# Block transposes over 128 partitions with a trip through HBM, in a float32r two-block transformer kernel

## The chip, the cores and the metric

The kernel runs on one core of a Trainium2 chip. The metric is the device time of one execution in microseconds; for the kernel before it is the median of three runs. Five engines take part, each with its own instruction queue: TensorE (PE; its weight loads are listed apart as PEld), VectorE (DVE), ScalarE (ACT), GpSimd (POOL) and SyncE (SP). SP, ACT and POOL also issue transfers, which all run on the same 16 DMA engines.

## The reference, cut to what matters

The input is one sequence of 256 tokens by 1024 channels, float32. It passes through two blocks of two layers each. Every layer of either block has the same frame:

```python
for l in range(2):
    x = x + 0.5 * swiglu(rms_norm(x, ffn1_norm[l]), ffn1_w_in[l], ffn1_w_out[l])
    x = x + mixer(rms_norm(x, mix_norm[l]), ...)
    x = x + 0.5 * swiglu(rms_norm(x, ffn2_norm[l]), ffn2_w_in[l], ffn2_w_out[l])

def swiglu(x, w_in, w_out):
    g, u = jnp.split(x @ w_in, 2, axis=-1)
    return (jax.nn.silu(g) * u) @ w_out
```

The FFN is 1024 to 2 x 2816 to 1024. The mixers differ: in the first block (mixer1 below) neighbourhood attention with a bias and a two-dimensional Fourier mix, both gated; in the second (mixer2) stick-breaking attention, compressed, selected and windowed attention, and top-k attention. So there are eight FFNs, two mixer1 and two mixer2.

## The kernel before, in words

The 256 tokens are two tiles of 128 (`T = 2`). A product `h @ w` has the tokens on the output's partitions: the activations are the stationary operand and must stand with channels on the partitions, so every activation that enters a product is first transposed. The weights are the moving operand, 512 columns at a time.

Float32 accuracy is had by splitting: `split` (L313) makes `hi`, a value rounded to float32r by ScalarE, and `lo = value - hi` by VectorE. `mm3` (L112) does three matmuls, hi x hi, hi x lo, lo x hi (L114, L115, L116).

`dense` (L118) is a product over `nk` slabs of 128 channels. For every four slabs it calls `unit` (L80), which issues one weight transfer of 1 MB on SP into one of four `raw` buffers and splits it in two pairs of slabs (tiles `whi` and `wlo` of 2 x 512 columns; two buffers in pools of their own and, in FFNs and mixer1, two more in the pool `big`, in mixer2 one more). A pair feeds 2 slabs x 2 token tiles x 3 = 12 matmuls.

Work that need not come at once is put in a list, `todo`: after each weight pair's split, `unit` takes up to `rate` entries off the list (L104 to L106), with the order kept behind that split; `drain` (L61) does the rest. The final order on each engine is set by a scheduler that goes by its own estimates, so that the list's order shifts somewhat.

`ffn` (L218): six chunks `c`, each with the gate and the up product (the sixth has both in one), then ScalarE's Silu out of the accumulators (`sl`, L246) and VectorE's product into `h` (L248). There are three accumulator buffers beside the four for attention, so the next chunk's matmuls need the evacuations. Chunks are grouped (0-1, 2-3, 4, 5); at a group's end `queue_t` (L65) puts the group's transposes on the list: 1024 columns (`nk = 8`) twice, then 512, then 256 for each token tile. `queue_blocks` (L179) makes 16 VectorE transposes for each token tile, each of one 32-partition row of blocks into 32 partitions of `hT`:

```python
hv[32 * qc : 32 * qc + 32, :, t * P + 32 * qa : t * P + 32 * qa + 32],
src[32 * qa : 32 * qa + 32, :nk, qc, :]
```

Then follow splits of `hT` into `hhi`, `hlo`, the stationary operands of the two output products (L252 on). After the first of these, half of `x` is final and is transposed in the same way by `queue_x` (L170); the other half goes over TensorE (`xt_half`, L187). `mixer1` (L432 on) does it for q and k (`qT`, `kT`). Mixer2 transposes on TensorE only, but for `queue_x` of its neighbours.

POOL has little to do: some memsets and the loads of small broadcast operands, among them the gate bias `h` in mixer1 (L518).

Of the kernel before, what the change touches and what calls it, by code (L numbers as in the profile page):

```python
# [10 lines left out]
F32 = mybir.dt.float32  # L11
# [7 lines left out]
P = 128  # L19
T = 2  # L20
# [6 lines left out]
class Net:  # L27
    def __init__(self, tc, ctx, a):
        self.tc, self.nc, self.a = tc, tc.nc, a
        nc = self.nc  # L30
        pool = lambda n, b, **kw: ctx.enter_context(tc.tile_pool(name=n, bufs=b, **kw))
# [9 lines left out]
        self.at = pool("at", 4, space=PS)  # L41
        self.tp = pool("tp", 1, space=PS)
        self.uid = 0
        self.flip = False
# [13 lines left out]
        self.hold = False  # L58
        self.todo, self.rate = [], 4

# [4 lines left out]
    def queue_t(self, h, nk, hhi, hlo, k0):  # L65
        hv = self.b("hT", n=2048)[:, : nk * 256].rearrange("p (k t) -> p k t", k=nk)
        for t in range(T):
            self.queue_blocks(h[t], nk, hv, t)
        for i in range(0, nk, 2):
            self.todo.append(lambda i=i: self.split(hhi[:, k0 + i : k0 + i + 2], hlo[:, k0 + i : k0 + i + 2],  # L70
                                                    hv[:, i : i + 2]))

# [97 lines left out]
    def queue_x(self, li):  # L170
        nc = self.nc
        hv = self.xtile()[:, :1024].rearrange("p (k t) -> p k t", k=4)
        for t in range(T):
            self.queue_blocks(self.x[:, t, :512], 4, hv, t)
        for k in range(4):
            g = self.gcol[:, li, k : k + 1] if isinstance(li, int) else li[:, k : k + 1]
            self.todo.append(lambda k=k, g=g: self.split(self.xhi[:, k], self.xlo[:, k], hv[:, k], scale=g))

    def queue_blocks(self, src, nk, hv, t):  # L179
        src = src.rearrange("p (k c i) -> p k c i", c=4, i=32)  # L180
        for q in range(16):
            qa, qc = q // 4, q % 4
            self.todo.append(lambda qa=qa, qc=qc: self.nc.vector.transpose(  # L183
                (hv(qc) if callable(hv) else hv)[32 * qc : 32 * qc + 32, :, t * P + 32 * qa : t * P + 32 * qa + 32],
                src[32 * qa : 32 * qa + 32, :nk, qc, :]))

# [196 lines left out]
class Mix1:  # L383
# [34 lines left out]
    def mixer1(self, l, nxt):  # L418
        nc, a, tc = self.nc, self.a, self.tc
# [3 lines left out]
        big = self.big  # L423
        self.more(2)
        tl = lambda n, sh, dt=F32: big.tile(sh, dt, name=self.nm(n), tag="m1" + n)
        kzh = big.tile([P, 4, 2, 256], F32R, name=self.nm("kzh"), tag="mlo")
        kq = big.tile([P, 4096], F32R, name=self.nm("kq"), tag="m1th")
        kzl = kq[:, :2048].rearrange("p (k i t) -> p k i t", k=4, i=2)
        ql = kq[:, 2048:3072].rearrange("p (k t) -> p k t", k=4)
        qT = big.tile([P, 4, 256], F32, name=self.nm("qT"), tag="m1fhi")  # L430
        kT = big.tile([P, 4, 256], F32, name=self.nm("kT"), tag="m1flo")
        qh, vn = tl("qh", [P, 4, 256], F32R), tl("vn", [P, T, 512])  # L432
# [6 lines left out]
        for c in range(4):  # L439
# [5 lines left out]
            if c < 2:  # L445
                h = []
                for t in range(T):
# [6 lines left out]
                    h.append(ht)  # L454
                for t in range(T):
                    self.queue_blocks(h[t], 4, qT if c == 0 else kT, t)
            elif c == 2:
# [12 lines left out]
        self.drain()  # L470
        self.split(qh, ql, qT)
        for i in range(2):
            r = slice(64 * i, 64 * i + 64)
            self.split(kzh[r, :, i, :], kzl[r, :, i, :], kT[r])
        ohi, olo = tl("ohi", [P, 4, 256], F32R), tl("olo", [P, 4, 256], F32R)
# [19 lines left out]
        for g in range(4):  # L495
            pa = self.psum(self.at)
            for tt in range(T):
                s = slice(g * P, (g + 1) * P)
# [5 lines left out]
            for q in range(2):  # L504
                s = slice(q * P, (q + 1) * P)
# [9 lines left out]
        for c in range(4):  # L515
# [4 lines left out]
            for t in range(T):  # L520
                d = th[:, t, c * 512 : (c + 1) * 512]
# [20 lines left out]
class Mix2:  # L542
    def consts2(self):
        nc, a = self.nc, self.a
# [9 lines left out]
        nc.scalar.dma_start(out=self.mc32[:, P:], in_=a["c2m"][:, 0:P])  # L554
        self.c2v = self.cst2.tile([P, 286], F32, name="c2v")
        nc.scalar.dma_start(out=self.c2v, in_=a["c2v"])
        v = self.c2v
# [6 lines left out]
        self.bmask = v[0:120, 278:286]  # L564
        self.one = self.cst2.tile([P, 1], F32, name="one")
        nc.gpsimd.memset(self.one, 1.0)
# [72 lines left out]
    def compress(self, l, kv, z, hid):  # L639
        nc, a = self.nc, self.a  # L640
# [19 lines left out]
        nc.tensor.transpose(ph[:, P : P + 30], th, self.ident[:30, :30])  # L660
        hT = self.b("chT", 30)
        nc.vector.tensor_copy(hT, ph[:, P : P + 30])
# [4 lines left out]
    def mixer2(self, l, nxt):  # L667
        nc, a = self.nc, self.a
# [4 lines left out]
        big = self.big  # L673
# [3 lines left out]
        tl = lambda n, sh, dt=F32, tag=None, bufs=1: big.tile(sh, dt, name=self.nm(n), tag=tag or "m2" + n, bufs=bufs)  # L677
# [16 lines left out]
        nc.gpsimd.memset(ikz, 0.0)  # L694
        kcz = tl("kcz", [P, 2, 15])
        nc.gpsimd.memset(kcz, 0.0)
# [134 lines left out]
        def cmp(t):  # L831
            sc = self.psum(self.at)
            for p in range(4):
                mm(sc[:, p * 30 : (p + 1) * 30], lhsT=nq[:, p, t * P : (t + 1) * P], rhs=flat(kcz), start=True, stop=True)
            pr = self.b("cpr", 120)
            pv3 = pr.rearrange("p (h c) -> p h c", h=8)
# [131 lines left out]
        for nm_, o, kk in (("a", oa, 2), ("b", ob, 4), ("c", oc, 2)):  # L968
# [4 lines left out]
            hi, lo = hl[:, :kk], hl[:, kk:]  # L973
# [6 lines left out]
        for n in range(2):  # L980
            for i, nm_ in enumerate("abc"):
                hi, lo, kk = oT[nm_]
                y = self.dense(hi, lo, kk, [(a[f"w_br_{nm_}_2"][l], n * 512, 512)])
                for t in range(T):
                    d, d0 = th[2 * i + n][:, t], th[n][:, t]
# [154 lines left out]
```

## Time and profile before

| | |
|---|---|
| median of 3 runs | 2369.55 us (2368.86 to 2369.81) |
| span of the profiled execution | 2366.5 us, first to last instruction |
| PE / PEld busy | 2291.0 us (97%) / 1846.8 us (78%) |
| DVE busy | 1891.9 us (80%) |
| ACT busy | 1144.7 us (48%) |
| POOL busy | 22.3 us (1%) |
| weight queue (q1) | 397.44 MB, 51.0% of 16 DMA engines' span |
[...]

The span is that of one execution on the chip; its own time is not listed apart from the three runs, whose lowest is 2.4 us above the span. Matmuls are pipelined: each is listed with some 390 ns while the next starts 227 ns after it, so a busy TensorE says that there was no gap longer than that overlap, and start-to-start distances say more. Times in the rows are microseconds unless marked ns. "A <- B: us, times, longest" in the view of waits says how long A's engine stood before A until B ended.

### The profile page before, as it was taken

The page shows a single profiled execution, that of the slowest core. Times are in us where ns is not written, and L with a number is a line of the kernel's source. Part 1 is how long each engine was busy: PE and PEld are TensorE (multiplying, and loading weights), DVE is VectorE, ACT ScalarE, POOL GpSimd, SP SyncE. Part 2 cuts the span into 40 slices and gives each one's busy share as a digit, 9 for nine tenths or more (in the row PEclk, how much of TensorE's full clock was granted, in tenths as well). Part 3 has the DMA queues.
Part 4 walks back from the last instruction along what each step waited for, and adds up shares of the span by engine and source line. Part 5 has one row for each costly group of instructions (what it writes and reads, how often), then busy time and mean ns, then how long its engine had stood idle before and what let it go on. Part 6 is the DMA issues. An engine that isn't in the chain of part 4 may idle for free.

```text
span 2366.5 us, 28600 instructions
## 1 busy us (share of the span) xinstructions
PE 2291.0 (97%) x10446; PEld 1846.8 (78%) x10446; DVE 1891.9 (80%) x3797; ACT 1144.7 (48%) x1632; POOL 22.3 (1%) x47
## 2 busy tenths in 40 slices
PE   8999999999999999999999999999999999999999
PEld 7777788778778788777777887787787788778777
DVE  6898866896798876798788896768958978877785
ACT  5444445445444455445444655544444455455443
POOL 0000000000000000000000000000000000000000
PEclk9999999999999999999999999999999999999999
DMA  7555555556546645546555544455464555325553
GB/s 257 177 171 185 177 170 178 173 174 201 182 151 200 191 152 178 189 142 219 176 175 179 174 125 132 137 185 182 166 211 161 173 191 156 124 96 189 185 177 117
DMA packets 228269, 407.07 MB, mean 172 GB/s; under 512 B 20800, under 2 KB 46016, under 8 KB 228128
## 3 DMA queue, kind: packets, MB, share of 16 engines
q1 hardware_dynamic: 212272, 397.44, 51.0%
q10 hardware_dynamic: 14944, 4.79, 0.9%
q0 software_dynamic: 912, 3.02, 0.5%
q8 instruction: 82, 1.34, 0.2%
q14 instruction: 59, 0.48, 0.1%
HBM read 404.16 MB, written 1.05 MB: 171 GB/s over the span
## 4 chain that ended last, share of the span: by engine, by line
PE 66%; DVE 27%; issue 5%; ACT 2%; DMA 1%; ACTq 0%; DVEq 0%
PE ps L115 20%; PE ps L116 20%; PE ps L114 19%; DVE hT L183 14%; DVE wlo L316 8%; DVE h L248 2%; PE ps L377 2%; DVE hlo L316 1%; ACT whi L315 1%; PE ps L370 1%; PE ps L863 1%; DVE qT L183 1%; PE ps L655 1%; DMA raw<-in_mix_w_in_dram 1%; PE ps L194 1%
## 5 line engine op out<-in xcount | busy, mean ns | idle before, releaser
L315 ACT CAST whi<-raw 128x1024 fp32r<-128x1024 f32 (+2 forms) x754 | 780.2, 1043 | 834.4 <-PE ps L116 744.8
L316 DVE TENSOR_TENSOR wlo<-raw,whi 128x1024 fp32r<-128x1024 f32 (+2 forms) x754 | 907.6, 1213 | 337.1 <-ACT whi L315 323.6
L115 PE MATMUL ps<-wlo,xhi 128*128 128x512 f32 (+2 forms) x2048 | 804.6, 394 | 14.7 <-DVE wlo L316 14.7
L114 PE MATMUL ps<-whi,xhi 128*128 128x512 f32 (+2 forms) x2048 | 772.4, 394 | 22.1 <-DVE h L248 18.9
L116 PE MATMUL ps<-whi,xlo 128*128 128x512 f32 (+2 forms) x2048 | 791.2, 390 | 0.0
L114 PEld LDWEIGHTS ps<-whi,xhi 128*128 128x128 f32 x2048 | 383.4, 188 | 112.7 <-DVE h L248 25.7
L115 PEld LDWEIGHTS ps<-wlo,xhi 128*128 128x128 f32 x2048 | 384.8, 188 | 110.5 <-DVE wlo L316 31.2
L116 PEld LDWEIGHTS ps<-whi,xlo 128*128 128x128 f32 x2048 | 384.8, 188 | 79.3 <-issue 0.5
L183 DVE STREAM_TRANSPOSE hT<-h 32x256 f32<-32x256 f32 (+2 forms) x1024 | 360.8, 352 | 15.4
L115 PE MATMUL ps<-wlo,hhi 128*128 128x512 f32 x704 | 279.1, 396 | 23.7 <-DVE wlo L316 23.7
L116 PE MATMUL ps<-whi,hlo 128*128 128x512 f32 x704 | 275.8, 392 | 0.0
L114 PE MATMUL ps<-whi,hhi 128*128 128x512 f32 x704 | 266.2, 392 | 1.1 <-DVE h L248 0.2
L115 PEld LDWEIGHTS ps<-wlo,hhi 128*128 128x128 f32 x704 | 132.1, 188 | 65.2 <-DVE wlo L316 37.5
L114 PEld LDWEIGHTS ps<-whi,hhi 128*128 128x128 f32 x704 | 132.2, 188 | 33.7 <-DVE h L248 4.6
L116 PEld LDWEIGHTS ps<-whi,hlo 128*128 128x128 f32 x704 | 132.2, 188 | 27.8
L315 ACT CAST hhi<-hT 128x512 fp32r<-128x512 f32 x88 | 49.1, 618 | 119.1 <-DVE hT L183 119.1
L246 ACT ACTIVATE sl<-ps,rstd 128x512 f32<-128x512 f32 (+1 forms) x96 | 62.3, 651 | 56.4 <-PE ps L116 52.3
L183 DVE STREAM_TRANSPOSE hT<-x 32x128 f32<-32x128 f32 x224 | 67.7, 302 | 3.4
L365 ACT ACTIVATE pr<-ms,nmx 128x256 f32<-128x256 f32 (+1 forms) x112 | 51.3, 461 | 34.0 <-DVE nmx L360 29.9
L248 DVE SCALAR_TENSOR_TENSOR h<-ps,rstd,sl 128x512 f32<-128x512 f32 (+1 forms) x96 | 64.7, 700 | 1.9 <-PE ps L116 1.6
L316 DVE TENSOR_TENSOR hlo<-hT,hhi 128x512 fp32r<-128x512 f32 x88 | 55.7, 685 | 0.3
L137 ACT ACTIVATE jk<-x 128x512 f32<-128x512 f32 x52 | 32.7, 630 | 5.3 <-DVE x L299 2.6
(350 smaller groups left out, 1681.7 us busy)
## 6 DMA issues: line engine op xcount, KB each, us to landing
raw<-in_ffn_w_gu_dram SPq DMA_DIRECT2D x80, 1024.0 KB, 5.1
raw<-in_ffn_w_in_dram SPq DMA_DIRECT2D x79, 1024.0 KB, 5.2
raw<-in_ffn_w_out_dram SPq DMA_DIRECT2D x40, 1024.0 KB, 5.0
raw<-in_ffn_w_down_dram SPq DMA_DIRECT2D x40, 1024.0 KB, 5.1
raw<-in_mix_w_in_dram SPq DMA_DIRECT2D x32, 1024.0 KB, 6.7
raw<-in_w_gate_dram SPq DMA_DIRECT2D x24, 1024.0 KB, 5.1
raw<-in_w_in_dram SPq DMA_DIRECT2D x12, 1024.0 KB, 5.5
raw<-in_ffn_w_in_dram SPq DMA_DIRECT2D x16, 512.0 KB, 4.6
```

The costliest lines, as they stand in the source:

```text
L114: mm(ps[:, :n], lhsT=lh, rhs=hi, start=start, stop=False)
L115: mm(ps[:, :n], lhsT=lh, rhs=lo, start=False, stop=False)
L116: mm(ps[:, :n], lhsT=ll, rhs=hi, start=False, stop=stop)
L137: self.nc.scalar.activation(junk, self.x[:, t, n * 512 : (n + 1) * 512], AF.Square, accum_out=ss[:, t, n : n + 1])
L183: self.todo.append(lambda qa=qa, qc=qc: self.nc.vector.transpose((hv(qc) if callable(hv) else hv)[32 * qc : 32 * qc + 32, :, t * P + 32 * ...
L194: nc.tensor.transpose(ps[:, j * 256 + t * P : j * 256 + (t + 1) * P], self.x[:, t, k * P : (k + 1) * P], self.ident)
L246: nc.scalar.activation(sl[:, :w], gs[t][:, :w], AF.Silu, scale=rs[:, t : t + 1])
L248: nc.vector.scalar_tensor_tensor(h[t][:, o : o + w], us[t][:, :w], rs[:, t : t + 1], sl[:, :w], op0=ALU.mult, op1=ALU.mult)
L315: self.nc.scalar.copy(hi, src)
L316: return self.nc.vector.tensor_sub(lo, src, hi.bitcast(F32))
L365: nc.scalar.activation(pr[:, s], src[:, s], AF.Exp, bias=nm[:, j : j + 1], accum_out=den[:, j : j + 1])
L377: nc.tensor.matmul(po[:, j * 64 : (j + 1) * 64], lhsT=pt[:, q], rhs=v(j, st), start=(st == 0), stop=(st == ns - 1))
```

## The change

- `queue_blocks` is gone. `turned` takes its place: for each token tile one VectorE transpose over all 128 partitions, which turns each 32 x 32 block in place and gathers the columns so that element `i` of a block is column `4 i + c` (the input steps by 4 elements). The result goes to `hB`, one buffer. After the second token tile, POOL issues a store of `hB` to a buffer in HBM (`hop`, two for each size) and a load back into the tile, which brings the rows to their partitions.
- Splits read the loaded tile in pieces of 32 columns; there are as many as before for 1024 and 512 columns, one more for 256; `queue_x` has 8 of 128 columns instead of 4 of 256; q has 2 in place of 1, k 4 in place of 2.
- Two empty entries (three in `queue_x`) stand in the list between the transposes and the splits, and `rate` is 1 instead of 4.
- Tiles of odd size are padded: `c2v` 286 to 288 columns, `one` 1 to 16, `kcz` 30 to 32, `chT` 30 to 32, `cpr` 120 to 128.

```diff
+        self.hop = pool("hop", 2, space=bass.MemoryType.DRAM)
...
-        self.todo, self.rate = [], 4
+        self.todo, self.rate = [], 1
...
     def queue_t(self, h, nk, hhi, hlo, k0):
-        hv = self.b("hT", n=2048)[:, : nk * 256].rearrange("p (k t) -> p k t", k=nk)
-        for t in range(T):
-            self.queue_blocks(h[t], nk, hv, t)
-        for i in range(0, nk, 2):
-            self.todo.append(lambda i=i: self.split(hhi[:, k0 + i : k0 + i + 2], hlo[:, k0 + i : k0 + i + 2],
-                                                    hv[:, i : i + 2]))
+        hv = self.turned(lambda t: h[t], nk, self.b("hT", n=2048))
+        self.todo += [lambda: None] * 2
+        step = min(nk, 4)
+        for i in range(0, nk, step):
+            for t in range(T):
+                o = lambda d: d[:, k0 + i : k0 + i + step, t * P : (t + 1) * P].rearrange(
+                    "p k (q j) -> p k q j", j=32)
+                self.todo.append(lambda hi=o(hhi), lo=o(hlo), s=hv[:, i : i + step, t]: self.split(hi, lo, s))
+
+    def turned(self, src, nk, tile):
+        nc = self.nc
+        n = nk * 256
+        hop = self.hop.tile([4, P, nk * 64], F32, name=self.nm("hop"), tag=f"hop{nk}")
+        hb = self.b("hB", n=2048, bufs=1)[:, :n]
+        ov = hb.rearrange("p (c k t j) -> p k c t j", c=4, t=T, j=32)
+
+        def turn(t):
+            nc.vector.transpose(ov[:, :, :, t, :], src(t)[:, : nk * P].rearrange("p (k i c) -> p k c i", c=4, i=32))
+            if t == T - 1:
+                nc.gpsimd.dma_start(out=hop.rearrange("q (i c) n -> (q i) (c n)", c=4), in_=hb)
+                nc.gpsimd.dma_start(out=tile[:, :n].rearrange("p (q n) -> p q n", q=4),
+                                    in_=hop.rearrange("q p n -> p q n"))
+
+        self.todo += [lambda t=t: turn(t) for t in range(T)]
+        return tile[:, :n].rearrange("p (q k t j) -> p k t q j", q=4, t=T, j=32)
...
     def queue_x(self, li):
...
+        hv = self.turned(lambda t: self.x[:, t, :512], 4, self.xtile())
+        self.todo += [lambda: None] * 3
...
-        self.c2v = self.cst2.tile([P, 286], F32, name="c2v")
-        nc.scalar.dma_start(out=self.c2v, in_=a["c2v"])
+        self.c2v = self.cst2.tile([P, 288], F32, name="c2v")
+        nc.scalar.dma_start(out=self.c2v[:, :286], in_=a["c2v"])
...
-        self.one = self.cst2.tile([P, 1], F32, name="one")
+        self.one = self.cst2.tile([P, 16], F32, name="one")[:, :1]
```

How it moves instructions, at two places. First VectorE in the first FFN, at the end of chunk 1: `h` are the chunk's two evacuations, `wlo` the low halves of the next weight pairs, `hlo` the low half of the transposed group. Before:

```order
L248 SCALAR_TENSOR_TENSOR h_333<-ps_411,rstd_304,sl_481 128x512
L248 SCALAR_TENSOR_TENSOR h_334<-ps_412,rstd_304,sl_484 128x512
L183 STREAM_TRANSPOSE hT_487<-h_333 32x8x32 x12
L316 TENSOR_TENSOR wlo_543<-raw_532,whi_542 128x1024
L183 STREAM_TRANSPOSE hT_487<-h_333 32x8x32 x4
L316 TENSOR_TENSOR wlo_579<-raw_576,whi_578 128x1024
L183 STREAM_TRANSPOSE hT_487<-h_334 32x8x32 x4
```

And now:

```order
L263 SCALAR_TENSOR_TENSOR h_335<-ps_413,rstd_306,sl_483 128x512
L263 SCALAR_TENSOR_TENSOR h_336<-ps_414,rstd_306,sl_486 128x512
L84 STREAM_TRANSPOSE hB_491<-h_335 128x8x4x32
L331 TENSOR_TENSOR wlo_539<-raw_532,whi_538 128x1024
L84 STREAM_TRANSPOSE hB_491<-h_336 128x8x4x32
L331 TENSOR_TENSOR wlo_571<-raw_568,whi_570 128x1024
L331 TENSOR_TENSOR wlo_577<-raw_568,whi_576 128x1024
L331 TENSOR_TENSOR wlo_609<-raw_606,whi_608 128x1024
L331 TENSOR_TENSOR wlo_615<-raw_606,whi_614 128x1024
L331 TENSOR_TENSOR wlo_657<-raw_654,whi_656 128x1024
L331 TENSOR_TENSOR hlo_151<-hT_489,hhi_150 128x4x128 x4
```

Thirty-two transposes in bursts of twelve and four became two, and five weight pairs stand between the second and the splits. On ScalarE the casts `hhi` of the same group stand, as before, in the middle of the weight casts:

```order
L330 CAST whi_614<-raw_606 128x1024
L261 ACTIVATE sl_649<-ps_493,rstd_306 128x512
L330 CAST whi_656<-raw_654 128x1024
L330 CAST hhi_150<-hT_489 128x4x128 x4
L330 CAST whi_660<-raw_654 128x1024
```

What they wait for is no longer VectorE but the load into `hT`. That load stands on POOL's queue, which holds now, for the first FFN and on into mixer1:

```order
L86 DMA hop_490<-hB_491 128x2048
L87 DMA hT_489<-hop_490 128x4x512
L86 DMA hop_799<-hB_800 128x2048
L87 DMA hT_798<-hop_799 128x4x512
L86 DMA hop_962<-hB_963 128x1024
L87 DMA hT_961<-hop_962 128x4x256
L86 DMA hop_1049<-hB_1050 128x512
L87 DMA hT_1048<-hop_1049 128x4x128
L86 DMA hop_1257<-hB_1258 128x1024
L87 DMA hT_1256<-hop_1257 128x4x256
```

Each load waits on POOL for its store; before, POOL had nothing at this place.

## Rows read from the trace of the kernel before

**Rows 1.** The page, part 1: busy us, share of the span, instructions.

```profile
PE 2291.0 (97%) x10446; PEld 1846.8 (78%) x10446; DVE 1891.9 (80%) x3797; ACT 1144.7 (48%) x1632; POOL 22.3 (1%) x47
```

**Rows 2.** Waits, whole span: us in total, times, longest us.

```profile
ACT whi L315 <- PE ps L116: 744.8, 485, 7.1
...
PE ps L115 <- DVE wlo L316: 38.4, 57, 1.7
...
PE ps L114 <- DVE h L248: 19.0, 17, 1.2
```

**Rows 3.** Chain of waits in 97 to 128 us, shares by line.

```profile
by line: DVE hT L183 44.4%; DVE wlo L316 19.7%; issue 13.9%; DVE hlo L316 8.0%; DVE h L248 6.4%; ACT whi L315 3.4%; PE ps L114 2.4%; PE ps L116 1.5%; PE ps L115 0.8%
```

**Rows 4.** Timeline of DVE from 97 us: start us, us, what.

```profile
99.44 1.40 DVE L248 SCALAR_TENSOR_TENSOR h<-ps,rstd,sl 128x512 f32<-128x512 f32 x2
100.76 5.36 DVE L183 STREAM_TRANSPOSE hT<-h 32x256 f32<-32x256 f32 x12
106.15 1.23 DVE L316 TENSOR_TENSOR wlo<-raw,whi 128x1024 fp32r<-128x1024 f32 x1
107.41 1.80 DVE L183 STREAM_TRANSPOSE hT<-h 32x256 f32<-32x256 f32 x4
```

**Rows 5.** Timeline of PE, a stretch without waits in either block's FFN.

```profile
590.02 0.39 PE L114 MATMUL ps<-whi,xhi 128*128 128x512 f32 x1
...
602.03 0.39 PE L116 MATMUL ps<-whi,xlo 128*128 128x512 f32 x1
...
1770.18 0.39 PE L115 MATMUL ps<-wlo,xhi 128*128 128x512 f32 x1
...
1780.84 0.39 PE L116 MATMUL ps<-whi,xlo 128*128 128x512 f32 x1
```

**Rows 6.** Timeline of PE from 121.5 us, with the idle time before.

```profile
121.77 0.39 PE L116 MATMUL ps<-whi,xlo 128*128 128x512 f32 x1
122.69 0.50 PE L115 MATMUL ps<-wlo,xhi 128*128 128x512 f32 x1 [0.53 <-DVE wlo L316]
...
125.31 0.39 PE L114 MATMUL ps<-whi,xhi 128*128 128x512 f32 x1
126.89 0.50 PE L114 MATMUL ps<-whi,xhi 128*128 128x512 f32 x1 [1.19 <-DVE h L248]
```

**Rows 7.** The page, part 5: transposes with all forms together.

```profile
L183 DVE STREAM_TRANSPOSE hT<-h 32x256 f32<-32x256 f32 (+2 forms) x1024 | 360.8, 352 | 15.4
...
L183 DVE STREAM_TRANSPOSE hT<-x 32x128 f32<-32x128 f32 x224 | 67.7, 302 | 3.4
```

**Rows 8.** Groups of DVE by form: xcount, busy us, mean ns, idle before.

```profile
L183 DVE STREAM_TRANSPOSE hT<-h 32x256 f32<-32x256 f32 x512 | 223.0, 435 | 7.7
L183 DVE STREAM_TRANSPOSE hT<-h 32x128 f32<-32x128 f32 x256 | 77.4, 302 | 3.8
```

**Rows 9.** Windows, two FFNs, one mixer2: PE, PEld, DVE, ACT, POOL busy, PEclk, DMA share, GB/s.

```profile
556.70:747.20 190.50, 183.80 (x802) 148.46 (x801) 155.35 (x276) 87.63 (x106) 0.72 (x1) 1.00 0.54 176
...
1734.50:1927.00 192.50, 186.64 (x801) 148.88 (x800) 155.20 (x274) 87.35 (x106) 0.17 (x1) 1.00 0.55 180
...
1927.00:2170.50 243.50, 242.68 (x1236) 196.40 (x1236) 195.65 (x548) 135.56 (x257) 4.21 (x11) 1.00 0.45 143
```

**Rows 10.** DMA: weight queue; landing of all `raw` loads, of POOL's gate bias loads.

```profile
q1 hardware_dynamic: 212272, 397.44, 51.0%
...
DMA to landing us min/median/max: 3.4/5.1/11.1
...
DMA to landing us min/median/max: 3.4/4.1/7.0
```

**Rows 11.** Groups of ACT by form: the casts.

```profile
L315 ACT CAST whi<-raw 128x1024 fp32r<-128x1024 f32 x734 | 765.3, 1051 | 819.9 <-PE ps L116 730.3 <-DMA raw<-in_mix_w_in_dram 37.2 <-DVE hT L183 18.8
...
L315 ACT CAST hhi<-hT 128x512 fp32r<-128x512 f32 x88 | 49.1, 618 | 119.1 <-DVE hT L183 119.1
```

More of the change, by code (lines that the diff above doesn't have):

```diff
@@ L170, in queue_x, with part @@
     def queue_x(self, li):
[L171 to L175, printed above, removed]
-            g = self.gcol[:, li, k : k + 1] if isinstance(li, int) else li[:, k : k + 1]
[L177 to L185, printed above, removed]
+        hv = self.turned(lambda t: self.x[:, t, :512], 4, self.xtile())
+        self.todo += [lambda: None] * 3
+        def part(k):
+            g = self.gcol[:, li, k : k + 1] if isinstance(li, int) else li[:, k : k + 1]
+            for t in range(T):
+                o = lambda d: d[:, k, t * P : (t + 1) * P].rearrange("p (q j) -> p q j", j=32)
+                self.split(o(self.xhi), o(self.xlo), hv[:, k, t], scale=g)
+        self.todo += [lambda k=k: part(k) for k in range(4)]
     def xt_half(self, n, li):
@@ L429, in mixer1 @@
         ql = kq[:, 2048:3072].rearrange("p (k t) -> p k t", k=4)
-        qT = big.tile([P, 4, 256], F32, name=self.nm("qT"), tag="m1fhi")
-        kT = big.tile([P, 4, 256], F32, name=self.nm("kT"), tag="m1flo")
+        qT = big.tile([P, 1024], F32, name=self.nm("qT"), tag="m1fhi")
+        kT = big.tile([P, 1024], F32, name=self.nm("kT"), tag="m1flo")
         qh, vn = tl("qh", [P, 4, 256], F32R), tl("vn", [P, T, 512])
@@ L454, in mixer1 @@
                     h.append(ht)
-                for t in range(T):
-                    self.queue_blocks(h[t], 4, qT if c == 0 else kT, t)
+                turned = self.turned(lambda t, h=h: h[t], 4, qT if c == 0 else kT)
+                qv, kv = (turned, None) if c == 0 else (qv, turned)
             elif c == 2:
@@ L470, in mixer1 @@
         self.drain()
[L471 to L474, printed above, removed]
+        for t in range(T):
+            o = lambda d: d[:, :, t * P : (t + 1) * P].rearrange("p k (q j) -> p k q j", j=32)
+            self.split(o(qh), o(ql), qv[:, :, t])
+            for i in range(2):
+                r = slice(64 * i, 64 * i + 64)
+                self.split(o(kzh[:, :, i])[r], o(kzl[:, :, i])[r], kv[r, :, t])
         ohi, olo = tl("ohi", [P, 4, 256], F32R), tl("olo", [P, 4, 256], F32R)
@@ L660, in compress @@
         nc.tensor.transpose(ph[:, P : P + 30], th, self.ident[:30, :30])
-        hT = self.b("chT", 30)
+        hT = self.b("chT", 32)[:, :30]
         nc.vector.tensor_copy(hT, ph[:, P : P + 30])
@@ L694, in mixer2 @@
         nc.gpsimd.memset(ikz, 0.0)
-        kcz = tl("kcz", [P, 2, 15])
+        kcz = tl("kcz", [P, 32])[:, :30].rearrange("p (g c) -> p g c", g=2)
         nc.gpsimd.memset(kcz, 0.0)
@@ L834, in cmp @@
                 mm(sc[:, p * 30 : (p + 1) * 30], lhsT=nq[:, p, t * P : (t + 1) * P], rhs=flat(kcz), start=True, stop=True)
-            pr = self.b("cpr", 120)
+            pr = self.b("cpr", 128)[:, :120]
             pv3 = pr.rearrange("p (h c) -> p h c", h=8)
```

## The prediction

> **What bounds the kernel now.** I read the page's busy line first. TensorE is busy for 2291.0 of 2366.5 us and VectorE for 1891.9 [rows 1]. At 97% TensorE is the bound over the whole span, so a faster VectorE is worth only what TensorE waits for it. That is in the view of waits: TensorE's two large ones are for `wlo`, the low half of a weight pair (38.4 us in 57 waits), and for `h`, the evacuation of its accumulators (19.0 us in 17) [rows 2]. Both are VectorE's work. ScalarE in turn waits 744.8 us for TensorE: its casts are held back by the weight buffers that TensorE frees, so in most stretches it runs ahead as far as the buffers allow.
>
> The chain of waits shows where VectorE is late. Between 97 and 128 us, in the first FFN, it is VectorE almost throughout: 44.4% block transposes, 19.7% `wlo`, and TensorE below 5% [rows 3]. VectorE's timeline in that stretch shows the pattern [rows 4]: after the two `h`, twelve transposes in one go (5.36 us), then four (1.80 us) beside each `wlo` (1.23 us). A weight pair feeds 12 matmuls, which start 0.2266 us apart (590.02 to 602.03 us, 53 steps) [rows 5], so a pair lasts TensorE 2.72 us, while VectorE needs 1.23 + 1.80 = 3.03 us for one. It falls behind until the transposes are through, and TensorE then stands twice. Start to start, 121.77 to 122.69 us is 0.92 us where 0.23 us is normal, so 0.69 us is lost though 0.53 us is printed as idle; 125.31 to 126.89 us loses 1.35 us against 1.19 us printed [rows 6]. Each wait thus loses 0.16 us more than printed, the tail of a matmul that otherwise overlaps. Over the kernel: 38.4 + 19.0 + 74 x 0.16 = **69 us lost to a late VectorE**.
>
> **What leaves VectorE.** Today's transposes take 360.8 + 67.7 us [rows 7] plus 128 more of 302 ns for q and k, 467 us together. Each fills 32 partitions. A transpose of 128 columns takes 302 ns and one of 256 takes 435 ns [rows 8], so 1.04 ns a column over a fixed 169 ns. The change issues 86: 32 of 1024 columns, 38 of 512, 16 of 256. If they keep that slope they take 1.23, 0.70 and 0.44 us: 39.5 + 26.6 + 7.0 = 73 us. VectorE loses some 394 us of work and TensorE's waits for it should nearly vanish: beside a `wlo` there is now at most one transpose, 1.23 + 1.23 = 2.46 us, under the 2.72 us of a pair. I count 62 of the 69 us; the rest lies at the start and in the mixers, where other work makes VectorE late.
>
> What could make the new transposes dearer is their input: element i of a block lies four columns behind element i-1, so reads step by 16 bytes, and the trace holds no VectorE read of SBUF with such a step. The bounds are the slope above and twice it, when a read yields half as much: 169 + 2 x 1065 = 2.30 us. I take 1.23 us for the sum, nearest to the measured transposes, and make the other a rival. [...]
>
> **What the padding does.** The two blocks run the same FFN. At 556.7 us (block 1) and 1734.5 us (block 2) VectorE has 155.35 and 155.20 us of work, the weight loads take the same, but TensorE is busy 183.80 and 186.64 us [rows 9]; its matmuls start 0.2317 us apart in block 2 (1770.18 to 1780.84 us, 46 steps) against 0.2266 us [rows 5]. Clock, shapes and order are alike; what differs is the place of the tiles. `c2v` has 286 columns, 1144 bytes, `one` 4 bytes, and everything allocated later in block 2 (in FFNs half of the weight pairs, `hhi`, `hlo`) starts 32 bytes off a multiple of 64; with 288 and 16 columns it does not. Four FFNs at 2.84 us are 11.4 us. Mixer2 has no twin; its TensorE is busy 242.68 of 243.50 us [rows 9], so a gain there would count in full, and with fewer misplaced operands I take 1 us each. Bounds 0 and 17 us, the latter with mixer2 gaining as much as an FFN; I count **13 us**.
>
> **What the trip through HBM adds.** 43 round trips, each a store and a dependent load on POOL's queue: 1 MB each way in 16 (eight FFNs, two groups), 0.5 MB in 19, 0.25 MB in 8, so 55 MB beside 397.44 MB of weights, which keep the 16 engines 51.0% busy [rows 10]. Weights have slack: four raw buffers, two pairs each. The risk is the order. The splits that use the result (`hhi` on ScalarE, `hlo` on VectorE) stand in the queues ahead of later weight casts, so a late landing stops the weights too; today ScalarE's 88 `hhi` casts wait 119.1 us for transposes [rows 11].
>
> The budget for 1 MB, counted from the last matmul of a chunk: the second transpose ends at about 5.1 us (`h` twice 1.40, transpose, `wlo`, transpose at 1.23 each). Five pairs lie between it and the splits. The cast of the fifth gets its buffer when TensorE has done five pairs of the new chunk, at 13.6 us, and takes 1.05 us [rows 11], so ScalarE can stand from 14.6 us on. TensorE needs the pair behind the splits at 9 x 2.72 = 24.5 us; before that ScalarE does four `hhi` (2.5 us) and a cast (1.05 us) and VectorE a `wlo` (1.2 us). The landing may therefore come until 19.7 us: **14.6 us for both transfers**. Beyond that TensorE loses each microsecond, 16 times over. For 0.5 MB the same count gives 11 to 13 us.
>
> The trip's length is not in the trace. The nearest rows: 1 MB of weights lands in 5.1 us at the median and 11.1 us at worst, and POOL's own 0.25 MB loads in 3.4 to 7.0 us [rows 10], the long ones with weights in flight. Two transfers give 10.2 to 22 us. I take 7 us each, 14 in all, because weights occupy the engines half of the time, and put the mean loss at 0.5 us per group: **8 us**. [...]
>
> The rest goes together: 28 more short splits on x, and TensorE's order, which changes only in which matmul of a pair comes first. Both are covered by VectorE's and ScalarE's new slack; without that cover 28 x 0.5 us on either would be 14 us.
>
> **Sum.** The span of 2366.5 us is 3 us under the median of 2369.55 us, and I take those 3 us as unchanged: 2369.5 - 62 - 13 + 8 = **2303 us**.
>
> **Rivals.**
> - *The strided transposes run at half rate.* 2.30 us each for 1024 columns; both end 2.1 us later, the budget falls to 12.5 us, and a trip of 14 us costs 1.5 to 2.5 us per group: 16 x 2 = 32 us instead of 8, some 6 us more at the half-megabyte groups: **2335 us**. For it: nothing in the trace reads SBUF this way. Against: VectorE's total stays far under its present one.
> - *The wait moves instead of going.* The chunks still lose their 62 us, to the landings in place of the transposes, and only the padding counts: **2356 us**. For it: 14 us against 14.6 us is no margin.
> - *The trips land far too late* (slower). One mechanism: the two transfers share the engines with the weights, ScalarE stands at the first `hhi` behind each 1 MB trip and TensorE runs out of pairs. It decides from the point where 16 x (trip - 14.6) outweighs 75 us, a trip of 19.3 us. At 21 us it is 16 x 6.4 = 102 us and the time **2397 us**. For it: weights in flight together took up to 11.1 us. Against: half of the weight loads land within 5.1 us, so several at once are not the rule.
> - *The padding does nothing*, as it would if something other than the address made block 2's matmuls slower: 2316 us, within the forecast's own range.
>
> **How the numbers follow.** Forecast 0.50, half rate 0.25, moved wait 0.12, late trips 0.13. What a measurement can tell from no change is 0.2%, 4.7 us. Faster: all of the first two, nearly all of the third: 0.86. Slower: most of the fourth: 0.11; within 0.2%: 0.03. The range begins at 2282 us (all 69 and 17 us gained, no stall) and reaches to 2350 us, over the half-rate case and part of the moved wait; what it leaves out is about 2 in 10. The forecast's own range is 2282 to 2320 us.
>
> **What would show it.** VectorE at some 1500 us busy; the 128-partition transposes at 1.23 us or 2.30 us; TensorE's waits for `wlo` and `h` mostly gone; FFNs of block 1 near 183 us, those of block 2 with matmuls 0.227 us apart as in block 1; ScalarE's waits before `hhi` now ended by a DMA. I am wrong if the 1 MB trips take over 19 us, if matmuls of block 2 stay at 0.232 us, or if TensorE's waits have another releaser and the same total.

## The result, and the profile after

| | before | after |
|---|---|---|
| median | 2369.2 us (2368.51 to 2369.81) | 2290.61 us (2284.74 to 2296.03) |
| span of the profiled execution | 2366.5 us | 2294.2 us (its time: 2296.03 us) |

The ratio is 0.967 (95% interval 0.9655 to 0.9678): 78.6 us less, where 66 us were forecast. The profiled execution is the slowest of the four after; numbers read from its trace are set against its own span.

The page's busy line, which answers to [rows 1]:

```profile
PE 2266.9 (99%) x10446; PEld 1857.2 (81%) x10446; DVE 1548.6 (67%) x2549; ACT 1149.2 (50%) x1674; POOL 78.1 (3%) x133
```

VectorE has 343 us less to do, not 394. The waits, which answer to [rows 2] and to the last row of [rows 11]:

```profile
ACT whi L330 <- PE ps L136: 740.0, 475, 7.6
...
ACT hhi L330 <- DMA hT<-hop: 84.4, 31, 6.5
...
PEld ps L135 <- DVE wlo L331: 15.8, 14, 3.4
...
PE ps L135 <- DVE wlo L331: 10.5, 12, 3.0
```

TensorE's wait for `h` has left the list and that for `wlo` fell from 38.4 to 10.5 us. ScalarE's wait ahead of `hhi` is now ended by a load and is shorter than before (84.4 against 119.1 us).

VectorE by form; these groups answer to [rows 7, 8] (count, busy us, mean ns):

```profile
L84 DVE STREAM_TRANSPOSE hB<-h 128x1024 f32<-128x1024 f32 x32 | 63.8, 1994 | 0.0
...
L84 DVE STREAM_TRANSPOSE hB<-h 128x512 f32<-128x512 f32 x24 | 25.1, 1084 | 0.0
...
L84 DVE STREAM_TRANSPOSE hB<-h 128x256 f32<-128x256 f32 x16 | 10.2, 637 | 0.9 <-DMA hop<-hB 0.6
```

The transposes are dearer than the forecast's 1.23, 0.70 and 0.44 us.

The place of [rows 4], at the end of chunk 1 of the first FFN: timelines of VectorE, POOL, ScalarE and TensorE (start us, us, what, idle before).

```profile
99.67 2.00 DVE L84 STREAM_TRANSPOSE hB<-h 128x1024 f32<-128x1024 f32 x1
101.60 1.18 DVE L331 TENSOR_TENSOR wlo<-raw,whi 128x1024 fp32r<-128x1024 f32 x1
102.69 1.98 DVE L84 STREAM_TRANSPOSE hB<-h 128x1024 f32<-128x1024 f32 x1
...
104.97 0.55 POOL L86 DMA_DIRECT2D hop<-hB  x1 [36.89 <-DVE hB L84]
111.14 0.76 POOL L87 DMA_DIRECT2D hT<-hop  x1 [5.62 <-DMA hop<-hB]
...
115.16 1.05 ACT L330 CAST whi<-raw 128x1024 fp32r<-128x1024 f32 x1 [3.80 <-PE ps L136]
119.95 2.18 ACT L330 CAST hhi<-hT 128x512 fp32r<-128x512 f32 x4 [3.74 <-DMA hT<-hop]
...
121.54 0.39 PE L136 MATMUL ps<-whi,xlo 128*128 128x512 f32 x1
123.14 0.50 PE L134 MATMUL ps<-whi,xhi 128*128 128x512 f32 x1 [1.21 <-ACT whi L330]
124.40 0.50 PE L135 MATMUL ps<-wlo,xhi 128*128 128x512 f32 x1 [0.76 <-DVE wlo L331]
```

The second transpose ends at 104.67 us. The load lands 15.3 us later. ScalarE has been free since 116.2 us (11.5 us after the transpose) and stands 3.74 us in front of `hhi`; the next weight cast is queued behind it, and TensorE loses 1.37 + 1.03 us against its usual distance of 0.23 us. This is the longest of the 16 trips of 1 MB. Read in the same way, they take 11.9 to 15.3 us, 13.2 us on average; TensorE loses nothing in the ten that take up to 13.2 us, and 0.4 to 2.4 us in each of the other six, 7.3 us together.

The page on the queues (packets, MB, share of 16 engines), which answers to [rows 10], and on the two transfers (median us from issue to landing):

```profile
q1 hardware_dynamic: 212272, 397.44, 51.7%
q0 software_dynamic: 14320, 60.69, 7.3%
...
hop<-hB POOLq DMA_DIRECT2D x16, 1024.0 KB, 5.7
hT<-hop POOLq DMA_DIRECT2D x16, 1024.0 KB, 6.6
```

In mixer1 the trip costs in another way. The chain of waits in 215 to 232 us (start us, us, what; "ACTq" is ScalarE's queue issuing a transfer):

```profile
215.14 6.78 DMA qT<-hop
...
221.95 1.14 ACT qh L330 x2
...
223.28 0.64 ACTq L426
...
223.95 4.66 DMA rawb<-in_rpbp_dram
...
229.35 1.23 DVE wlo L331
```

ScalarE issues the loads of the bias tables. The four loads of the second table stand in its queue behind the cast `qh`, which waits for q's trip, so they go out late; VectorE waits for them with three `wlo` behind, and TensorE stands for 2.99 us. How much this costs differs between executions: counted between the same matmuls, the two mixer1 take 326.0 us together in this one, but 317.9 us in same_place and 318.1 us in no_padding, which make the same trips, and 315.8 us in no_trip, which makes none (all three below).

The two FFNs of [rows 9], and a stretch of block 2 that answers to the second half of [rows 5]:

```profile
538.53:721.63 183.10, 181.16 (x802) 149.31 (x801) 115.12 (x130) 88.02 (x111) 7.27 (x11) 1.00 0.65 220
1678.14:1862.51 184.37, 183.77 (x802) 149.24 (x801) 115.15 (x130) 87.89 (x111) 6.99 (x11) 1.00 0.66 225
```

```profile
1759.82 0.39 PE L136 MATMUL ps<-whi,xlo 128*128 128x512 f32 x1
...
1771.83 0.39 PE L134 MATMUL ps<-whi,xhi 128*128 128x512 f32 x1
```

Block 2's FFN is still 2.6 us busier on TensorE: 52 steps in 12.01 us are 0.2310 us, against 0.2317 us before and 0.2266 us in block 1. **The padding did not do what the prediction said.**

### The profile page after: what moved, and what is told of

The parts are those of the page before. It is cut to its first block, busy times and chain, and to the rows that moved or that the text cites. A ratio compares the mean times of both kernels' runs of the same rounds, so it can differ in the third digit from the quotient of the medians.

```text
span 2294.2 us, 27621 instructions
## 1 busy us (share of the span) xinstructions
PE 2266.9 (99%) x10446; PEld 1857.2 (81%) x10446; DVE 1548.6 (67%) x2549; ACT 1149.2 (50%) x1674; POOL 78.1 (3%) x133
## 4 chain that ended last, share of the span: by engine, by line
PE 71%; issue 20%; DMA 6%; DVE 2%; ACT 1%; ACTq 0%; DVEq 0%; POOLq 0%; POOL 0%
PE ps L135 22%; PE ps L134 22%; PE ps L136 22%; DMA hT<-hop 2%; DMA hop<-hB 2%; PE ps L392 1%; DVE wlo L331 1%; DVE hlo L331 1%; PE ps L385 1%; DMA qT<-hop 1%; ACT whi L330 1%; PE ps L209 1%; PE ps L880 0%; DMA rawb<-in_rpbp_dram 0%; PE ps L672 0%
## 5 line engine op out<-in xcount | busy, mean ns | idle before, releaser
L135 PE MATMUL ps<-wlo,xhi 128*128 128x512 f32 (+2 forms) x2048 | 801.1, 393 | 10.3 <-DVE wlo L331 10.3
L134 PE MATMUL ps<-whi,xhi 128*128 128x512 f32 (+2 forms) x2048 | 786.5, 393 | 3.7 <-ACT whi L330 3.4
L135 PE MATMUL ps<-wlo,hhi 128*128 128x512 f32 x704 | 274.2, 389 | 0.2 <-DVE wlo L331 0.2
L134 PE MATMUL ps<-whi,hhi 128*128 128x512 f32 x704 | 273.1, 392 | 0.0
L84 DVE STREAM_TRANSPOSE hB<-h 128x1024 f32<-128x1024 f32 (+2 forms) x72 | 99.0, 1389 | 0.9 <-DMA hop<-hB 0.6
L331 DVE TENSOR_TENSOR hlo<-hT,hhi 128x512 fp32r<-128x512 f32 (+1 forms) x96 | 57.0, 642 | 57.4 <-ACT hhi L330 57.3
L330 ACT CAST hhi<-hT 128x512 fp32r<-128x512 f32 (+1 forms) x96 | 49.8, 582 | 84.5 <-DMA hT<-hop 84.4
L86 POOL DMA_DIRECT2D hop<-hB x43 | 23.5, 546 | 1757.5 <-DVE hB L84 746.3
L87 POOL DMA_DIRECT2D hT<-hop x39 | 29.5, 757 | 184.4 <-DMA hop<-hB 111.9
```

The source lines that it names most:

```text
L84: nc.vector.transpose(ov[:, :, :, t, :], src(t)[:, : nk * P].rearrange("p (k i c) -> p k c i", c=4, i=32))
L86: nc.gpsimd.dma_start(out=hop.rearrange("q (i c) n -> (q i) (c n)", c=4), in_=hb)
L87: nc.gpsimd.dma_start(out=tile[:, :n].rearrange("p (q n) -> p q n", q=4), in_=hop.rearrange("q p n -> p q n"))
L134: mm(ps[:, :n], lhsT=lh, rhs=hi, start=start, stop=False)
L135: mm(ps[:, :n], lhsT=lh, rhs=lo, start=False, stop=False)
L330: self.nc.scalar.copy(hi, src)
```

## The experiments

In the program before, operands of block 2 stood 32 bytes off a multiple of 64; now all stand at multiples of 64. But `xhi`, `xlo` and block 1's buffers stand at 64 modulo 128, and half of block 2's buffers at 0 modulo 128. The first four kernels test whether that is what counts, and what the trip costs.

**same_place**: block 2's buffers brought to the place of `xhi`, modulo 128.

```diff
-        self.one = self.cst2.tile([P, 16], F32, name="one")[:, :1]
+        self.one = self.cst2.tile([P, 32], F32, name="one")[:, :1]
```

> The changed kernel with `one` padded to 32 columns instead of 16, so that everything allocated behind it in block 2 moves by 64 bytes; it computes the same. Theory A (a matmul is slower when its moving and its stationary operand stand at different places modulo 128 bytes; the changed kernel put block 2's buffers 64 bytes off those of xhi and xlo): matmuls of block 2's FFNs go from 0.231 to 0.227 us apart, its four FFNs from 184 to about 181.5 us, and the time falls by 9 to 12 us. Theory B (64-byte multiples are all that matters, and something else in block 2, its weights for instance, makes it slower): no change, 0 +- 2 us, and 0.231 us stays.

Measured: 2279.45 us (2276.13 to 2281.89), 11.2 us less than the change; against before 0.962 (0.9606 to 0.9633). In block 2, TensorE's timeline:

```profile
1744.68 0.39 PE L136 MATMUL ps<-whi,xlo 128*128 128x512 f32 x1
...
1756.92 0.39 PE L136 MATMUL ps<-whi,xlo 128*128 128x512 f32 x1
```

54 steps in 12.24 us, 0.2267 us: block 1's distance, as theory A has it.

**block1_off**: the opposite, 64 bytes put ahead of block 1's buffers.

```diff
             with tc.tile_pool(name="cst1", bufs=1) as self.cst1:
+                self.cst1.tile([P, 16], F32, name="off64")
```

> The changed kernel with 64 unused bytes in the constants of block 1, so that block 1's buffers stand 64 bytes off those of xhi and xlo, as block 2's do; it computes the same. Theory A (different places modulo 128 bytes): the FFNs of block 1 get the 0.231 to 0.233 us of block 2, +8 to +11 us in all. Theory B (block 2 is slower for another reason): no change, 0 +- 2 us, block 1 stays at 0.227 us.

Measured: 2298.23 us (2297.36 to 2300.06), 7.6 us more than the change, just under the range expected. A stretch of block 1:

```profile
560.84 0.39 PE L135 MATMUL ps<-wlo,xhi 128*128 128x512 f32 x1
...
572.83 0.40 PE L136 MATMUL ps<-whi,xlo 128*128 128x512 f32 x1
```

52 steps in 11.99 us, 0.2306 us where it was 0.2266. Block 1 gets block 2's distance when it gets its places; neither the weights nor the code of block 2 are the cause.

**no_padding**: transposes and trip alone.

```diff
-        self.c2v = self.cst2.tile([P, 288], F32, name="c2v")
-        nc.scalar.dma_start(out=self.c2v[:, :286], in_=a["c2v"])
+        self.c2v = self.cst2.tile([P, 286], F32, name="c2v")
+        nc.scalar.dma_start(out=self.c2v, in_=a["c2v"])
...
-        self.one = self.cst2.tile([P, 16], F32, name="one")[:, :1]
+        self.one = self.cst2.tile([P, 1], F32, name="one")
...
```

> The changed kernel with the tiles of odd size as they were (286, 1, 30, 30 and 120 columns): transposes and trip alone. By the prediction's reason the padding was worth 13 us, so this should be 13 us slower than the changed kernel. By theory A (only the difference modulo 128 bytes counts, and both 32 and 64 bytes of difference are slow) the padding did almost nothing: +1 to +4 us, with matmuls of block 2 still 0.231 us apart.

Measured: 2291.99 us (2288.54 to 2294.72), 1.4 us more than the change, which the two ranges do not tell from nothing. The padding is worth a few microseconds at most, not 13.

**no_trip**: the transposes write where the splits read; the exchange of rows between partitions is left out.

```diff
-        hb = self.b("hB", n=2048, bufs=1)[:, :n]
+        hb = tile[:, :n]
...
-            if t == T - 1:
-                nc.gpsimd.dma_start(out=hop.rearrange("q (i c) n -> (q i) (c n)", c=4), in_=hb)
-                nc.gpsimd.dma_start(out=tile[:, :n].rearrange("p (q n) -> p q n", q=4),
-                                    in_=hop.rearrange("q p n -> p q n"))
```

> The changed kernel without the store to HBM and the load back: the transposes write into the tile that the splits read, so rows stay on the partitions where the transposes left them; this leaves out the exchange of rows between partitions. The prediction's 8 us for the trip, read in the changed kernel's trace as some 6.4 us behind late loads of hT and some 6 us of mixer1's bias loads behind other transfers, should go: 8 to 12 us less. Rival (the trips are hidden and the waits come from something else): 0 +- 2 us, with TensorE's waits for whi and wlo unchanged.

Measured: 2280.09 us (2279.83 to 2280.86), 10.5 us less. Of TensorE's long waits for a `wlo` one line is left in the view of waits (us in total, times, longest):

```profile
PEld ps L129 <- DVE wlo L325: 3.7, 5, 1.1
```

So the trip costs 10.5 us, and the transposes alone, with the padding's 1.4 us taken off, 2369.1 - 2280.1 - 1.4 = 87.6 us less than the old ones. Both are net of what the other order does: no_trip's second mixer2 takes 247.8 us, against 243.9 us in the change, with a wait there that the change does not have:

```profile
2049.12 0.52 PE L128 MATMUL ps<-whi,oTc 128*128 128x512 f32 x1 [2.10 <-ACT oTc L224]
```

So a trip without that side effect may be worth some 4 us more than the net.

**before_place**: the kernel before with the padding that same_place has, and nothing else.

```diff
-        self.c2v = self.cst2.tile([P, 286], F32, name="c2v")
+        self.c2v = self.cst2.tile([P, 288], F32, name="c2v")
...
-        self.one = self.cst2.tile([P, 1], F32, name="one")
+        self.one = self.cst2.tile([P, 32], F32, name="one")[:, :1]
...
```

> The kernel before with nothing but padding, and that padded so that block 2's buffers stand at the same place modulo 128 bytes as xhi and xlo (one to 32 columns, c2v to 288, the small tiles as in the change). Theory A: block 2's matmuls go from 0.232 to 0.227 us apart; over 2,800 of them at 2.6 to 6.6 ns that is 16 us at most, some of it lost again where TensorE waits for VectorE anyway: 8 to 14 us less, 2355 to 2361 us. If padding only pays once VectorE is out of the way: 0 to 3 us less.

Measured: 2360.08 us (2358.99 to 2363.07) against 2369.71 us, ratio 0.9961 (0.9948 to 0.9975): 9.6 us less. The right place pays with a late VectorE too, and by nearly as much.

**all_zero**: is it the place itself, or that both operands share it?

```diff
+        self.cst.tile([P, 16], F32, name="off64")
         self.ident = self.cst.tile([P, P], F32, name="ident")
```

> The kernel same_place with 64 unused bytes ahead of xhi and xlo, so that every operand of either block's products stands at a multiple of 128 bytes instead of 64 bytes past one; it computes the same. If what counts is that the two operands of a matmul stand at the same place modulo 128 bytes: no change against same_place's 2279 us, +- 3 us, 0.227 us in the FFNs of both blocks. If the place itself counts (64 past a multiple is good, a multiple bad): both blocks at 0.231 us, some 18 us more, 2297 us.

Measured: 2281.33 us (2276.06 to 2283.84), same_place within its range. The two operands have to agree in their place: both at 64 and both at 0 modulo 128 bytes are equally fast.

These kernels moved buffers by 32 or 64 bytes, so they cannot tell 128 bytes from a larger period. The addresses that the programs give their buffers, set against the starts of all the products' matmuls, can. By the distance between the moving and the stationary operand modulo 256 bytes, this is the time to the next matmul (us, mean of all distances under 0.3 us):

```
moving - stationary    0         64        128       192       32, 96, 160, 224
no_padding             0.2278    -         0.2332    -         0.2328 to 0.2339
change                 0.2277    0.2301    0.2318    0.2333    -
same_place             0.2271    -         0.2321    -         -
all_zero               0.2271    -         0.2321    -         -
```

In the FFNs of block 2 about half of the matmuls are off, so that 0.231 us is an average of both kinds. A distance of 128 bytes is slow as well: what has to agree is the place modulo 256 bytes, not 128. In same_place such matmuls are left in mixer2 alone (252 of 620 in either; in the second, 0.2321 us against 0.2295 us for the others there). No kernel moved them, so this part is read from traces and not tested.

**plain_read**: the transposes' input step; the columns that then stand in the wrong place are left there.

```diff
-            nc.vector.transpose(ov[:, :, :, t, :], src(t)[:, : nk * P].rearrange("p (k i c) -> p k c i", c=4, i=32))
+            nc.vector.transpose(ov[:, :, :, t, :], src(t)[:, : nk * P].rearrange("p (k c i) -> p k c i", c=4, i=32))
```

> The changed kernel with transposes that read their columns in order instead of every fourth (input step of 4 bytes instead of 16); the columns that then stand in the wrong place are left so, everything else is unchanged and in the same order. If the 16-byte step is what makes the transposes slow: 1.23, 0.70 and 0.44 us instead of 1.99, 1.08 and 0.64, VectorE some 50 us less busy. Time: by the theory that VectorE now has slack, only the trips gain, which start 1.5 us earlier: 0 to 5 us less. By the prediction's rival (half rate costs 32 us): some 20 us less or more.

Measured: 2286.58 us (2285.57 to 2288.54), 4.0 us less and within the change's own range. VectorE by form:

```profile
L84 DVE STREAM_TRANSPOSE hB<-h 128x1024 f32<-128x1024 f32 x32 | 39.5, 1234 | 0.0
...
L84 DVE STREAM_TRANSPOSE hB<-h 128x512 f32<-128x512 f32 x24 | 15.6, 686 | 0.0
...
L84 DVE STREAM_TRANSPOSE hB<-h 128x256 f32<-128x256 f32 x16 | 7.1, 441 | 1.6 <-DMA hop<-hB 1.4
```

These are the forecast's durations. Between 512 and 1024 columns a column costs (1234 - 686) / 512 = 1.07 ns, and with the step (1994 - 1084) / 512 = 1.78 ns. VectorE has 1507.1 us of work instead of 1548.6: 41.5 us less of it are worth 4 us of time or nothing, for now it has slack.

**long_trip**: the trip made twice.

```diff
                                     in_=hop.rearrange("q p n -> p q n"))
+                far = hop.rearrange("q p n -> p q n")
+                nc.gpsimd.dma_start(out=far, in_=tile[:, :n].rearrange("p (q n) -> p q n", q=4))
+                nc.gpsimd.dma_start(out=tile[:, :n].rearrange("p (q n) -> p q n", q=4), in_=far)
```

> The changed kernel with the trip made twice: after the load, the tile is stored to HBM and loaded again, so 12 to 16 us more for 1 MB; it computes the same. The scheduler puts the splits ten weight pairs behind the transposes instead of five, by its own estimate of the transfers. By the prediction's price (16 groups, every microsecond beyond the 14.6 us budget lost): some 220 us more. By the theory that the trip is hidden as long as the splits stand behind it in the queues: 0 to 40 us more, from q, k and x, whose users come soon.

Measured: 2372.64 us (2364.88 to 2381.19), 82 us more: between the two. ScalarE and TensorE at the second 1 MB trip:

```profile
129.28 1.06 ACT L333 CAST whi<-raw 128x1024 fp32r<-128x1024 f32 x1 [0.30 <-PE ps L139]
136.18 2.18 ACT L333 CAST hhi<-hT 128x512 fp32r<-128x512 f32 x4 [5.85 <-DMA hT<-hop]
...
135.65 0.39 PE L139 MATMUL ps<-whi,hlo 128*128 128x512 f32 x1
139.35 0.50 PE L137 MATMUL ps<-whi,hhi 128*128 128x512 f32 x1 [3.32 <-ACT whi L333]
```

The split now comes due 23.8 us after the second transpose instead of 11.5, since the scheduler moved it, but the trips take 24.3 to 29.9 us. TensorE loses up to 4.5 us in a group, 28.8 us in the 16. The mean granted clock is 0.988, which over 2368 us is, by an estimate from these two figures, at most another 28 us. The rest was not taken apart; counted between the same matmuls, 71 of the 74 us between the two profiled executions lie in the stretches of the FFNs, the first of which has the program's start with it.

**direct**: one transfer between partitions instead of two through HBM, on same_place.

```diff
-                nc.gpsimd.dma_start(out=hop.rearrange("q (i c) n -> (q i) (c n)", c=4), in_=hb)
-                nc.gpsimd.dma_start(out=tile[:, :n].rearrange("p (q n) -> p q n", q=4),
-                                    in_=hop.rearrange("q p n -> p q n"))
+                for q in range(4):
+                    nc.gpsimd.dma_start(out=tile[:, q * nk * 64 : (q + 1) * nk * 64],
+                                        in_=hb[32 * q : 32 * q + 32, :].rearrange("i (c n) -> i c n", c=4))
```

> The kernel same_place with the two transfers through HBM replaced by four from SBUF to SBUF (one for each 32 partitions of hB, a quarter of the tile each) on the same queue; it computes the same. If the length of the trip is what costs the 10 us that no_trip showed: the second latency goes, landings come 5 to 7 us earlier and the time falls from 2279 to 2269 to 2274 us. If transfers between partitions are slower than those with HBM, or four issues take POOL as long as two: 2279 us or more.

Measured: 2276.95 us (2276.4 to 2279.97), 2.5 us under same_place and short of the range expected. The 1 MB groups land 8.0 to 11.2 us after the transpose and cost TensorE nothing, but the scheduler, with shorter transfers to plan for, orders mixer2 differently: TensorE loses 2.2 us waiting for `oTc` there, in either mixer2, which it does not in same_place, and once 4.2 us for an `h` behind a late landing of 0.5 MB.

**near_h**: direct transfers for the FFNs' groups alone, on same_place.

```diff
-        hv = self.turned(lambda t: h[t], nk, self.b("hT", n=2048))
+        hv = self.turned(lambda t: h[t], nk, self.b("hT", n=2048), True)
...
-            if t == T - 1:
+            if t == T - 1 and near:
+                for q in range(4):
+                    nc.gpsimd.dma_start(out=tile[:, q * nk * 64 : (q + 1) * nk * 64],
+                                        in_=hb[32 * q : 32 * q + 32, :].rearrange("i (c n) -> i c n", c=4))
+            elif t == T - 1:
```

> The kernel same_place with the transfers from SBUF to SBUF of direct for the FFNs' groups alone; q, k and x keep the trip through HBM, with which mixer2's order on ScalarE stays that of same_place. It computes the same. If direct gained in the FFNs what its trace shows (180.5 us for each against 180.5 to 184.6) and lost it again to the other order in mixer2 (TensorE waits 2.4 us for oTc, twice): 2266 to 2273 us. If the FFNs' gain was that run's alone: 2277 us or more.

Measured: 2267.16 us (2265.63 to 2268.08), against before 0.9567 (0.9554 to 0.958), 23.5 us less than the change and **the fastest here**. Its page on the transfer, and its windows of an FFN of either block:

```profile
hT<-hB POOLq DMA_DIRECT2D x64, 256.0 KB, 6.1
```

```profile
529.50:709.98 180.48, 180.48 (x802) 149.54 (x801) 115.19 (x130) 88.25 (x112) 10.92 (x20) 1.00 0.65 207
1664.20:1844.70 180.50, 180.50 (x802) 149.47 (x801) 114.14 (x131) 87.99 (x112) 14.36 (x29) 1.00 0.67 214
```

TensorE has no idle time left in these FFNs, and the blocks are alike.

**plain_rows**: fast transposes, with the store sorting the rows, on same_place.

```diff
-"p (k i c) -> p k c i", c=4, i=32
+"p (k c i) -> p k c i", c=4, i=32
...
-                nc.gpsimd.dma_start(out=hop.rearrange("q (i c) n -> (q i) (c n)", c=4), in_=hb)
+                for q in range(4):
+                    nc.gpsimd.dma_start(out=hop[q].rearrange("(c i) n -> i c n", c=4),
+                                        in_=hb[32 * q : 32 * q + 32].rearrange("i (c n) -> i c n", c=4))
```

> The kernel same_place with transposes that read their columns in order, as in plain_read, and the store to HBM putting the rows where they belong (row c x 32 + i instead of 4 i + c, in four stores with pieces of 2 KB instead of 8 KB for the groups of 1024 columns); it computes the same. If VectorE's slack and the earlier start are all that counts: 2279 us less the 4 us of plain_read, 2275 us. If the smaller pieces and three more issues on POOL lengthen the trip by more than 1.5 us: 2279 us or more.

Measured: 2340.12 us (2334.46 to 2341.19), 61 us more than same_place: the second case, by far more than it had in mind. Its transfers:

```profile
hop<-hB POOLq DMA_DIRECT2D x64, 256.0 KB, 5.0
hT<-hop POOLq DMA_DIRECT2D x16, 1024.0 KB, 9.2
```

The load of 1 MB takes 9.2 instead of 6.6 us and the landing comes 16.1 to 19.3 us after the transpose, with the split due at 13.05 us: ScalarE stands 3.1 to 6.2 us in each of the 16 groups and TensorE loses some 1.33 us less than that each time, 51 us in all; the mean granted clock, 0.988 against 0.999 in same_place, adds to it. The step in the transposes, which costs 4 us or less, buys long pieces in the store. Why the load, whose own pieces are the same, takes longer as well was not tried.

## Why the prediction was right, and where its terms were not

The time lay 12.4 us below the forecast and within its range (whose lower end its own terms put at 2283.5 us, not 2282). The sum came out closer than its terms, and that is luck: the transposes were worth 26 us more than forecast, the padding 12 us less.

| term | forecast | measured | by |
|---|---|---|---|
| transposes leave VectorE | -62 us | -87.6 us | no_trip less no_padding's 1.4 us |
| padding | -13 us | -1.4 us | no_padding |
| trip | +8 us | +10.5 us | no_trip |
| together | -67 us | -78.5 us | change: -78.6 us |

The last line is no check of the others: the transposes' term is what the two other measured terms leave of the whole. It also holds what the list's order does (`rate` 1 instead of 4, the empty entries, the pieces of the splits), which no kernel varied by itself.

- **The late VectorE**: the mechanism holds, the size was too small. Worked out from all starts of the products' matmuls, what they take beyond 0.227 us is:

```
distance to the next    before             change             no_trip
over 0.4 us             102x, 81.1 us      43x, 23.5 us       25x, 8.6 us
0.3 to 0.4 us           220x, 22.0 us      129x, 12.0 us      126x, 11.7 us
```

In the first line lie the 69 us that the prediction counted, of which it took 62 as recovered; without the trip 72.5 us of the line went. The second was missed: the matmul behind a wait is slow too. In the prediction's own example the matmul that starts at 122.69 us [rows 6] is followed by the next at 123.02 us, 0.33 us instead of 0.23, so a wait costs another 0.10 us; 10.3 us of these went. The 5 us that are left sit in distances under 0.3 us; their cause was not tried.
- **The padding**: the failed step is "starts 32 bytes off a multiple of 64; with 288 and 16 columns it does not". The address was indeed the cause, but the condition was wrong: what counts is whether a matmul's two operands stand at the same place (same_place, block1_off, all_zero), by the traces modulo 256 bytes. The change turned distances of odd multiples of 32 bytes into odd multiples of 64, which is little better. With the right padding the term is worth 12.5 us (no_padding less same_place), near the 13 us forecast. Mixer2's share (1 us each) is hardly seen: the second lasts 242.8 us in same_place against 243.5 us before, with matmuls 0.231 us apart as ever; 252 of its 620 are still 128 bytes off, as the table under all_zero shows.
- **The trip**: 14 us were taken for 1 MB, 13.2 us measured; half a microsecond per group, 8 us, were taken for TensorE's loss, 7.3 us measured, from a few late landings, as the prediction had it. The budget of 14.6 us was nearer 13: ScalarE was free 11.5 us after the second transpose. Of the other 3 us or so some 2 lie where the prediction did not look, mixer1's bias loads behind `qh` (no_padding and same_place against no_trip). Each of the two transfers of 1 MB was taken at 7 us; issue to landing, the rows above show 5.7 us for the store and 6.6 us for the load at the median.
- **The half-rate rival** was right on the condition, nearly (1.99 against 2.30 us), and wrong on the price: 32 us were counted over the forecast (its terms add up to 30, 2333 us), plain_read shows 4 us or less. Its budget of 12.5 us was about right, but the trips took 13.2 us, not 14, and what misses the budget by less than a microsecond costs as little.
- **The late-trip rival**: its mechanism is what long_trip and plain_rows show, ScalarE standing and TensorE out of pairs, at one microsecond for each beyond 1.33 us of ScalarE's wait in plain_rows. Its fixed point of 19.3 us is not there: the scheduler puts the splits where it expects the landing, four pairs behind the transposes in direct, five in the change and ten in long_trip. As far as these kernels show, the loss comes from the error of that estimate, not from the length of the trip.

## What to carry to other kernels

When two pieces of code do the same at different speed, compare the addresses of a matmul's two operands modulo 256 bytes: 64 bytes of padding were worth 11 us here, and padding to multiples of 64 bytes 1.4 us, which the ranges do not tell from nothing. A transfer that a scheduler plans for can stand in a kernel's dependent chain if it lands as planned; shorten it (one transfer between partitions instead of two through HBM: near_h, 12.3 us under same_place) rather than make its pieces smaller (plain_rows, 61 us over it), and look at what is queued behind the instruction that waits for it (here mixer1's bias loads, and a stall of 2.99 us). Count a stall of TensorE by start-to-start distances over the stall and the matmul behind it: here 0.26 us more than the idle time printed.

## What the runs showed of the hardware

- From one 128x512 float32r matmul to the next it is 0.227 us if the moving and the stationary operand stand at the same place modulo 256 bytes (same_place, all_zero), and 0.230 to 0.234 us if they do not (change, no_padding); over an FFN in which half of them do not, 0.231 us.
- A VectorE transpose takes 1.07 ns a column between 512 and 1024 columns with its input in order (plain_read) and 1.78 ns with an input step of 16 bytes (change): 1.66 times as long, less than twice.
- The granted clock, 1.00 through the whole kernel before, is 0.50 for 3.4 us at two places of the change's profiled execution, from 231.9 and from 2044.4 us on. Five-microsecond windows of the change behind the stall of 2.99 us (PEclk is the column behind the busy times):

```profile
225.00:230.00 5.00, 2.63 (x12) 1.86 (x10) 1.53 (x2) 4.09 (x5) 0.76 (x1) 1.00 1.02 217
230.00:235.00 5.00, 4.38 (x13) 3.49 (x14) 4.62 (x5) 0.00 (x0) 0.00 (x0) 0.69 0.95 290
```

In the first of the two dips matmuls start 0.427 us apart: eight matmuls at 0.2 us more each, 1.6 us on top of the stall. A stall of 2.78 us at 759 us in the same run has no such dip, and TensorE's longest wait in the 14 us ahead of the second is 0.57 us; when a dip comes was not settled.
